# A two-layer decoder trunk on one core: matmul streams that take turns by whole chunks, an earlier weight load, and gates tied behind casts

## The chip, the cores and the metric

One NeuronCore of a Trainium2 chip runs the whole program. The metric is the device time of one execution in microseconds (us); lower is better. Before the change the median of three runs is 2906.79 us (2905.42 to 2907.09).

## The reference, cut to what matters

All matrices are float32; 256 positions, model width 2048, feed-forward width 5632.

```python
# layer 0
hn  = rmsnorm(h)
q, k, v, z, a, b, c_q, c_kv, k_rope = split_cols(hn @ w_in, L0_SPLITS)      # w_in: 2048 x 5200
y_a = gated_deltanet(q, k, v, z, a, b, ...)    # gates: sigmoid(b), softplus(a), cumulative decay
y_b = mla(c_q, c_kv, k_rope, cos, sin, ...)    # low-rank attention with rotary keys
h   = h + concat(y_a, y_b) @ w_out
h   = h + conv_ffn(rmsnorm(h))
h   = h + (p[0] @ w_proj) * sigmoid(rmsnorm(h) @ w_gate)
# layer 1: the same with retention in place of the mixer, then a final rmsnorm

def conv_ffn(hn, w_up, conv_w, conv_b, w_down):     # w_up: 2048 x 11264, w_down: 5632 x 2048
    u = causal_dwconv(hn @ w_up, conv_w) + conv_b   # width 3 along the positions
    gate, up = split(u, 2)
    return (silu(gate) * up) @ w_down
```

## The kernel before, in words

**Three matmuls for one.** Each float32 product is made of parts: a weight tile `raw` is cast to a rounded `hi` on ScalarE (L186) and the difference `lo = raw - hi` is taken on VectorE (L187). Activations are split the same way into tiles `xg`. TensorE then adds `hi` times both parts of x and `lo` times the high part. `cut` makes the casts and differences of one weight chunk; `split` takes a chunk that was loaded early from the list `ahead`, or loads one now through SyncE's DMA queue (L167), and cuts it. A chunk of weights is 1 MB (0.75 MB in the opening) and is cut into two `hi` and two `lo` tiles. There are four buffers for `raw`, four for `hi` and four for `lo`.

**Generators and steps.** The matmul loops are Python generators; each `yield` ends a step. `gemm_b` (up projection, transposed result) does a chunk of 1024 x 256 weights in three steps: 16 hi matmuls of 512 columns in two steps (L262), then 16 lo matmuls of 256 columns (L267); two chunks make one column block, which `joined` and `conv` then take through the causal convolution (L274 to L277, L1065, L1067). `gemm_a` does a chunk of 512 x 512 in three steps: 16 hi matmuls in two steps (L291, L292) and 8 lo matmuls (L297), all of 512 columns. After each step `turn()` runs one small deferred piece from the list `todo`, behind the last matmul.

**Order of issue.** The program's text gives the dependences and a priority. The framework in which it is written decides the order of the instructions on each engine by when its own model of the chip finds them ready; on the chip each engine then goes through its list in that order. `tc.issue_after(ins)` ties what is written inside it behind `ins` on the engine of `ins`.

**Feed-forward.** `ffn` goes over the 44 blocks of 128 hidden columns in groups: 4, then five times 8. While a group's `up` runs, the `down` of the group before it is worked off in turns with it. For four of the groups in each layer half of the output columns are done by `seven`: seven half-size products in place of eight (a fast-multiplication scheme), over sums of weight quadrants that GpSimd's accumulating DMA (L407) and two VectorE additions (L467) make. One `product` has three steps: two with four hi matmuls (L438, L439) and a cut each, one with four lo matmuls (L443). The other half of the columns is done by `plain`, four chunks of `gemm_a`. So `up` of a group has 48 steps, and the `down` beside it 12 plain and 21 product steps. `forms` are the sums of activation quadrants that the products need; they are made on VectorE (L376 to L384) each time two column pairs are ready.

Before, the two parts of `down` give one plain step, then two product steps, in turns; `up` first does `LAG` = 6 steps, and then after each single step of `up` the counter `owed` grows by `SHARE` = 0.85, and one step of `down` runs whenever it reaches 1.

**Opening.** The first product of layer 0 (16 blocks of x by 368 columns of `w_in`, four chunks) starts while x arrives. Its chunk 0 is loaded early into `ahead`; in the loop over the four column quarters of x, the two x tiles of the quarter after next are asked for at the loop's head, and the next chunk of weights only when `first_gemm` gets to it. `n0.feed` transposes x tiles (L311) and scales and splits them (L315, L316). Then come a second and a third product of the same kind (`g3` = 1 and 2). While they run, `turn()` works off `todo`: the scale's broadcast, two empty pieces, the five steps of `gates()` (L597 to L635: sigmoid, softplus, decay, with two changes of ScalarE's function table), a copy, the nine steps of `rope_steps` (L499 to L521), and so on. The results of a product are copied out of PSUM by `r_copy` (L576).

Of the kernel before, what the change touches and what calls it, by code (L numbers as in the profile page):

```python
# [13 lines left out]
F32 = mybir.dt.float32  # L14
# [16 lines left out]
WB = 4  # L31
PSA = 2
PSB = 4
LAG = 6
SHARE = 0.85
RATES = [1.7, 1.1, 1.1, 0.95, 2.8]
D = 2048
S = 256
# [2 lines left out]
CG = 4  # L41
# [43 lines left out]
def trunk(ctx: ExitStack, tc: tile.TileContext, a: dict):  # L85
# [12 lines left out]
    V, A, G, T = nc.vector, nc.scalar, nc.gpsimd, nc.tensor  # L98
    cnt = [0]

    def nm(s):
        cnt[0] += 1
        return f"{s}_{cnt[0]}"

    def t2(shape=(P, 512), dt=F32):
        return tp.tile(list(shape), dt, tag="t2", name=nm("t2"))
# [27 lines left out]
    def load_x(i, c, q=nc.sync):  # L134
        h[i][c] = t2()
        q.dma_start(h[i][c], a["x"][i * P : (i + 1) * P, c * 512 : (c + 1) * 512])
# [20 lines left out]

    grain = [GRAIN0]
    last_cast = [None]
    ahead = []  # L160

    def load(src, k, n, parts=1):
        raw = rawp.tile([P, k, n], F32, tag="raw", name=nm("raw"))
        rows = src.rearrange("(k p) n -> p k n", p=P)
        for q in range(0, k, k // parts):
            c = slice(q, q + k // parts)
            nc.sync.dma_start(raw[:, c], rows[:, c])  # L167
        return raw

    def split(src, k, n, views=None):  # L170
        raw = ahead.pop() if ahead else load(src, k, n)
        return cut(raw, k, n, views)

    def cut(raw, k, n, views=None):
        his, los = [], []
        step = max(1, PIECE // n)
        for k0 in range(0, k, step):
            kp = min(step, k - k0)
            hi = wp.tile([P, kp, n], F32R, tag="hi", name=nm("hi"))
            lo = wp.tile([P, kp, n], F32R, tag="lo", name=nm("lo"))  # L180
            rk = raw[:, k0 : k0 + kp]
            fine = max(1, grain[0] // n)
            for q in range(0, kp, fine):
                c = slice(q, min(q + fine, kp))
                for vi, vo in views or [(lambda t: t, lambda t: t)]:
                    last_cast[0] = A.copy(vo(hi)[:, c], vi(rk)[:, c])  # L186
                    V.tensor_sub(vo(lo)[:, c], vi(rk)[:, c], vo(hi)[:, c].bitcast(F32))  # L187
            his += [hi[:, i] for i in range(kp)]
            los += [lo[:, i] for i in range(kp)]
        return his, los  # L190
# [11 lines left out]
    def behind(step):  # L202

        with tc.issue_after(last_mm[0].ins):
            return step()

    def later(*steps):
        todo.extend(steps)

    def stepwise(gen, n):  # L210
        later(*[partial(next, gen, None)] * n)

    def turn():
        if todo:
# [38 lines left out]
    def gemm_b(w, c0, tiles):  # L253
        ps = pa()
        for c in range(2):
            hi, lo = split(w[c * 1024 : (c + 1) * 1024, c0 : c0 + 256], 8, 256)
            for j in range(2):
                for k in range(8):
                    x2, xh = xr(tiles, c * 8 + k)
                    wh = hi[k][:, j * P : (j + 1) * P]  # L260
                    first = c == 0 and k == 0
                    last_mm[0] = T.matmul(ps[:, j], wh, x2, start=first, stop=False)  # L262
                turn()
                yield
            for j in range(2):
                for k in range(8):
                    last_mm[0] = T.matmul(ps[:, j, :S], lo[k][:, j * P : (j + 1) * P], xr(tiles, c * 8 + k)[1], start=False, stop=c == 1 and k == 7)  # L267
            turn()
            yield
        return ps  # L270
# [259 lines left out]
    def idle(n):  # L530
        ps = pb()
        for _ in range(n):
            T.matmul(ps[:, :P], ones, ones, start=True, stop=True)
# [5 lines left out]
    w_in = a["l0_w_in"]  # L539
# [8 lines left out]
    n0.feed(0)  # L548
    idle(IDLE[1])
    for c in range(CG):  # L550
        if c < CG - 2:
            for i in range(NH):
                load_x(i, c + 2)
        next(first_gemm)
        if c > 0:
            with tc.issue_after(last_cast[0].ins):
                Norm.squares(n0, c - 1)
        if c < CG - 1:
            behind(partial(n0.feed, c + 1))
        for _ in range(2):  # L560
            next(first_gemm)
# [442 lines left out]
    n = Norm(C_NORM["l0_ffn_norm"])  # L1004
# [44 lines left out]
    def ffn(l, nf, nxt, aside=None):  # L1049
        pin = []  # L1050
        w_up, w_dn = a[f"l{l}_ffn_w_up"], a[f"l{l}_ffn_w_down"]
        fp = cp.tile([P, N_FFN], F32, name=nm("fp"), tag="fp")
        nc.sync.dma_start(fp, a["par"][:, N_PAR0 + l * N_FFN : N_PAR0 + (l + 1) * N_FFN])
        Xf = nf.tiles

        def fc(c):
            return fp[:, c : c + 1]

        def conv(cb, j0):
            ps = yield from gemm_b(w_up, cb, Xf)  # L1060
            u = joined(ps, nf.bc)
            y = t2((P, 2, S))
            for j in range(2):
                ct = j0 + j
                A.activation(y[:, j], u[:, j], AF.Identity, scale=fc(ct + 176), bias=fc(ct + 264))  # L1065
                for lag in range(1, 3):
                    V.scalar_tensor_tensor(y[:, j, lag:], u[:, j, : S - lag], fc(ct + (2 - lag) * 88), y[:, j, lag:], op0=ALU.mult, op1=ALU.add)  # L1067
            return y

        def up(g0, g1, tiles, forms):  # L1070
            kept = []
            for jp in range(g0, g1, 2):
                tiles.append(xtile())
                yg = yield from conv(jp * P, jp)
                yu = yield from conv(D_FF + jp * P, NFT + jp)
                A.activation(yg, yg, AF.Silu)
                V.tensor_mul(yg, yg, yu)
                put_split(tiles[-1], 0, 2, yg)
                if forms is not None:
                    kept.append(yg)  # L1080
                    if len(kept) == 2:
                        forms.add(*kept)
                        kept = []

        def down(g0, g1, tiles, forms, quads, then):
            r0, nk = g0 * P, g1 - g0

            def plain(cols):
                for c in cols:
                    ps = [pb() for _ in range(NH)]  # L1090
                    yield from gemm_a(w_dn, r0, nk, c * 512, 512, tiles, ps)
                    for i in range(NH):
                        V.tensor_add(h[i][c], h[i][c], ps[i])

            if forms is None:
                then()
                yield from plain(range(CG))
                return
            fast = seven(quads, tiles, forms, then)
            slow = plain(range(2, CG))  # L1100
            while next(slow, fast) is not fast:
                yield
                for _ in range(2):
                    if next(fast, slow) is not slow:
                        yield
            yield from fast

        groups = [(max(g - 4, 0), g + 4) for g in range(0, NFT, 8)]
        prev = None
        total = []  # L1110

        def following(g0):
            if g0 + 8 < NFT:
                if not total:
                    total.extend(running())
                quads.append(Quads(w_dn, g0 * P, 0, total))
                quads[-1].begin()

        quads = []
        for g0, g1 in groups:  # L1120
            forms = Forms() if 0 < g0 and g1 < NFT else None
            cur = (g0, g1, [], forms)
            going = up(g0, g1, cur[2], forms)
            if prev is not None:
                behind_it = down(*prev, quads[-1] if quads else None, partial(following, g0))
                for _ in range(LAG):
                    next(going)
                owed = 0.0
                for _ in going:
                    owed += SHARE  # L1130
                    while owed >= 1.0:
                        owed -= 1.0
                        next(behind_it, None)
                run(behind_it)
            else:
                run(going)
            if g0 == 4 and aside is not None:
                aside()
            if g1 + 8 == NFT:
                pin.append(ple_input(l))  # L1140
            prev = cur
        later(lambda: pin.append(ple_tiles(pin.pop())))
        run(proj_add(w_dn, [(prev[0] * P, prev[2], prev[1] - prev[0])], range(CG), nxt.feed))
        later(nxt.finish)
        return pin[0]
# [337 lines left out]
```

## Time and profile before

| | |
|---|---|
| median of three runs | 2906.79 us |
| profiled execution | 2905.5 us, span 2903.7 us |
| TensorE matmul (PE) busy | 2879.7 us, 15076 matmuls |
| TensorE weight load (PEld) busy | 2457.5 us |
| VectorE (DVE) busy | 2067.7 us |
| ScalarE (ACT) busy | 1539.3 us |
| DMA | 562.49 MB, mean 194 GB/s |
| granted TensorE clock, mean | 0.998 |

A line of the profile names an engine, a line of the kernel (L187), the operation, the tile written and those read, and a count. In a timeline the first two numbers are the start in us from the span's start and the length in us; a bracket at the end tells how long the engine stood idle before it, and what it waited for. Rows of matmuls are merged as `x16`, with the overlap of the last one in their length. "SPq" is SyncE's issue of a DMA. In the list of windows each row is one stretch: its length, then busy time and number of instructions of each engine, the granted TensorE clock as a share of full speed, and the DMA's share and rate.

### The profile page before, as it was taken

What the parts mean: (1) busy time and instruction counts of PE and PEld (TensorE: products, weight loads), DVE (VectorE), ACT (ScalarE), POOL (GpSimd) and SP (SyncE); (2) the same over time, 40 slices, a digit from 0 to 9 for tenths busy, and PEclk for the clock granted to TensorE, in tenths of its full rate; (3) what the DMA queues carried; (4) which work ended last, traced back from release to release, by engine and by line L of the source; (5) the groups of instructions that cost most, each with busy time, mean ns of one, the idle gap of its engine ahead of it and who ended that gap; (6) DMA issues with size and microseconds to landing.
All of it is one profiled execution on the core that took longest, in us unless ns stands there. A gap on an engine that the chain in (4) does not pass through costs nothing.

```text
span 2903.7 us, 38666 instructions
## 1 busy us (share of the span) xinstructions
PE 2879.7 (99%) x15076; PEld 2457.5 (85%) x15076; DVE 2067.7 (71%) x2898; ACT 1539.3 (53%) x2185; POOL 121.6 (4%) x116
## 2 busy tenths in 40 slices
PE   8999999999999999999999999999999999999998
PEld 8899988888888888888888888888888888888887
DVE  6878867777887877756565565655667878787865
ACT  6666655555555555554444444444545555555554
POOL 0111100000000000000000000000000000000000
PEclk9999999999999999999999999999999999999999
DMA  6444456657777777555555555555565777777654
GB/s 217 141 141 128 128 167 196 218 189 203 233 202 230 233 214 226 184 181 191 185 183 184 193 183 181 184 185 189 180 218 178 228 209 241 220 222 220 214 183 147
DMA packets 410040, 562.49 MB, mean 194 GB/s; under 512 B 10752, under 2 KB 266880, under 8 KB 409856
## 3 DMA queue, kind: packets, MB, share of 16 engines
q1 hardware_dynamic: 393376, 530.05, 55.8%
q0 software_dynamic: 13056, 25.17, 5.4%
q10 hardware_dynamic: 3424, 4.79, 0.5%
q8 instruction: 118, 1.93, 0.3%
q14 instruction: 66, 0.54, 0.1%
HBM read 557.87 MB, written 2.10 MB: 193 GB/s over the span
## 4 chain that ended last, share of the span: by engine, by line
PE 92%; DVE 4%; DMA 1%; issue 1%; ACT 1%; POOL 0%; SPq 0%; ACTq 0%; POOLq 0%; DVEq 0%
PE pa L262 28%; PE pa L267 15%; PE pa L291 10%; PE pa L292 10%; PE pa L297 10%; PE pb L292 2%; PE pb L291 2%; PE pb L297 2%; DVE lo L187 2%; PE pb L732 2%; PE pb L438 2%; PE pb L439 1%; PE pb L443 1%; PE pb L311 1%; DMA raw<-in_l_ffn_w_down_dram 1%
## 5 line engine op out<-in xcount | busy, mean ns | idle before, releaser
L187 DVE TENSOR_TENSOR lo<-raw,hi 128x1024 fp32r<-128x1024 f32 (+3 forms) x1140 | 1192.3, 1075 | 576.5 <-ACT hi L186 399.1
L186 ACT CAST hi<-raw 128x1024 fp32r<-128x1024 f32 (+3 forms) x1140 | 1014.4, 931 | 937.2 <-PE pa L292 327.9
L262 PE MATMUL pa<-xg,hi 128*128 128x512 f32 x3840 | 950.8, 393 | 0.0
L262 PEld LDWEIGHTS pa<-xg,hi 128*128 128x128 f32 x3840 | 705.8, 188 | 146.5 <-ACT hi L186 8.3
L291 PE MATMUL pa<-hi,xg 128*128 128x512 f32 (+1 forms) x1348 | 523.5, 389 | 7.2 <-ACT hi L186 7.1
L267 PEld LDWEIGHTS pa<-xg,lo 128*128 128x128 f32 x3840 | 495.0, 191 | 34.6 <-DVE lo L187 14.6
L292 PE MATMUL pa<-hi,xg 128*128 128x512 f32 (+1 forms) x1348 | 520.9, 387 | 0.3 <-DVE xg L316 0.2
L267 PE MATMUL pa<-xg,lo 128*128 128x256 f32 x3840 | 514.7, 284 | 1.5 <-DVE lo L187 1.2
L297 PE MATMUL pa<-lo,xg 128*128 128x512 f32 (+1 forms) x1348 | 332.6, 387 | 0.0
L291 PEld LDWEIGHTS pa<-hi,xg 128*128 128x128 f32 x1348 | 253.9, 188 | 56.9 <-ACT hi L186 7.7
L292 PEld LDWEIGHTS pa<-hi,xg 128*128 128x128 f32 x1348 | 254.0, 188 | 49.0 <-DVE xg L316 0.8
L297 PEld LDWEIGHTS pa<-lo,xg 128*128 128x128 f32 x1348 | 249.8, 188 | 47.5
L1067 DVE SCALAR_TENSOR_TENSOR t<-t,fp,t 128x255 f32<-128x255 f32 (+1 forms) x352 | 158.4, 480 | 54.1 <-ACT t L1065 50.7
L292 PE MATMUL pb<-hi,xg 128*128 128x512 f32 x348 | 135.9, 390 | 0.0
L291 PE MATMUL pb<-hi,xg 128*128 128x512 f32 x348 | 135.7, 390 | 0.0
L274 ACT COPY t<-pa 128x512 f32<-128x512 f32 x128 | 74.9, 585 | 100.9 <-PE pa L267 91.6
L1065 ACT ACTIVATE t<-t,fp 128x256 f32<-128x256 f32 x176 | 96.0, 593 | 48.0 <-DVE t L277 48.0
L407 POOL DMA_DIRECT2D xg<-in_l_ffn_w_down_dram x48 | 57.9, 1206 | 1185.4 <-DVE t L1067 395.5
L297 PE MATMUL pb<-lo,xg 128*128 128x512 f32 x348 | 92.4, 391 | 0.0
L275 DVE TENSOR_TENSOR t<-t,pa 128x512 f32<-128x512 f32 x128 | 87.1, 680 | 3.8 <-ACT t L274 3.8
L156 POOL TENSOR_TENSOR small<-small,mhalf 128x1 f32<-128x1 f32 (+2 forms) x38 | 28.6, 752 | 1415.3 <-DVE small L1252 622.6
L316 DVE SCALAR_TENSOR_TENSOR xg<-pb,par,xg 128x256 fp32r<-128x256 f32 x136 | 59.7, 479 | 35.9 <-ACT xg L315 35.5
(280 smaller groups left out, 2236.1 us busy)
## 6 DMA issues: line engine op xcount, KB each, us to landing
raw<-in_l_ffn_w_up_dram SPq DMA_DIRECT2D x176, 1024.0 KB, 5.6
raw<-in_l_w_in_dram SPq DMA_DIRECT2D x128, 1024.0 KB, 5.1
raw<-in_l_ffn_w_down_dram SPq DMA_DIRECT2D x56, 1024.0 KB, 5.3
raw<-in_l_w_out_dram SPq DMA_DIRECT2D x44, 1024.0 KB, 5.1
raw<-in_l_ffn_w_down_dram SPq DMA_DIRECT2D x64, 512.0 KB, 4.9
raw<-in_l_ple_gate_dram SPq DMA_DIRECT2D x32, 1024.0 KB, 5.1
xg<-in_l_ffn_w_down_dram POOLq DMA_DIRECT2D x48, 512.0 KB, 6.0
xg<-in_l_ffn_w_down_dram SPq DMA_DIRECT2D x16, 512.0 KB, 4.6
```

Of the source, the lines that this page charges most:

```text
L186: last_cast[0] = A.copy(vo(hi)[:, c], vi(rk)[:, c])
L187: V.tensor_sub(vo(lo)[:, c], vi(rk)[:, c], vo(hi)[:, c].bitcast(F32))
L262: last_mm[0] = T.matmul(ps[:, j], wh, x2, start=first, stop=False)
L267: last_mm[0] = T.matmul(ps[:, j, :S], lo[k][:, j * P : (j + 1) * P], xr(tiles, c * 8 + k)[1], start=False, stop=c == 1 and k == 7)
L274: A.copy(u, ps[:, :, S:])
L275: V.tensor_add(u, u, ps[:, :, :S])
L291: T.matmul(o[i], xh, hi[k], start=begin and k0 + k == 0, stop=False)
L292: last_mm[0] = T.matmul(o[i], xw, hi[k], start=False, stop=False)
L297: last_mm[0] = T.matmul(o[i], xl(tiles, k0 + k, i)[0], lo[k], start=False, stop=end and k0 + k == nkb - 1)
L316: V.scalar_tensor_tensor(t[:, kk, 1], pk, g, t[:, kk, 0].bitcast(F32), op0=ALU.mult, op1=ALU.subtract)
L1065: A.activation(y[:, j], u[:, j], AF.Identity, scale=fc(ct + 176), bias=fc(ct + 264))
L1067: V.scalar_tensor_tensor(y[:, j, lag:], u[:, j, : S - lag], fc(ct + (2 - lag) * 88), y[:, j, lag:], op0=ALU.mult, op1=ALU.add)
```

## The change

Four edits go together. (1) In `down`, the plain part and the product part take turns of `UNIT` = 3 steps, that is a whole chunk or a whole product: one plain, two products. (2) In the loop over groups, `down` gets its turn only after each third step of `up` (a whole up chunk), and then three steps of it; `LAG` is 2 chunks (6 steps as before) and `SHARE` 0.8. (3) In the opening, the next chunk of weights is loaded into `ahead` before the x tiles of the quarter after next; `ahead` becomes a queue that is taken from the left. (4) `cut` also keeps its last difference in `last_diff`, and `stepwise`, which serves `gates` and `rope_steps` in layer 0, ties each step behind the last cast on ScalarE and the last difference on VectorE that are written by then.

```diff
-LAG = 6
-SHARE = 0.85
+UNIT = 3
+LAG = 2
+SHARE = 0.8
...
-    ahead = []
+    last_diff = [None]
+    ahead = deque()
...
-        raw = ahead.pop() if ahead else load(src, k, n)
+        raw = ahead.popleft() if ahead else load(src, k, n)
...
-                    V.tensor_sub(vo(lo)[:, c], vi(rk)[:, c], vo(hi)[:, c].bitcast(F32))
+                    last_diff[0] = V.tensor_sub(vo(lo)[:, c], vi(rk)[:, c], vo(hi)[:, c].bitcast(F32))
...
     def stepwise(gen, n):
-        later(*[partial(next, gen, None)] * n)
+        def step():
+            with tc.issue_after(last_cast[0].ins), tc.issue_after(last_diff[0].ins):
+                next(gen, None)
+        later(*[step] * n)
...
     for c in range(CG):
+        if c < CG - 1:
+            ahead.append(load(w_in[(c + 1) * 512 : (c + 2) * 512, 4096 : 4096 + 368], 4, 368))
         if c < CG - 2:
             for i in range(NH):
                 load_x(i, c + 2)
...
             slow = plain(range(2, CG))
-            while next(slow, fast) is not fast:
-                yield
-                for _ in range(2):
-                    if next(fast, slow) is not slow:
-                        yield
-            yield from fast
+            going = True
+            while going:
+                going = False
+                for part in (slow, fast, fast):
+                    for _ in range(UNIT):
+                        if next(part, part) is not part:
+                            going = True
+                            yield
...
-                for _ in range(LAG):
+                for _ in range(LAG * UNIT):
                     next(going)
                 owed = 0.0
-                for _ in going:
+                for n, _ in enumerate(going, 1):
+                    if n % UNIT:
+                        continue
                     owed += SHARE
-                    while owed >= 1.0:
+                    if owed >= 1.0:
                         owed -= 1.0
-                        next(behind_it, None)
+                        for _ in range(UNIT):
+                            next(behind_it, None)
                 run(behind_it)
```

## The prediction

> **What bounds the kernel now.** I read the page first (engine shares, the chain that ended last), then windows by stage, then the timeline where PE pauses. A time is us from the span's start.
>
> ```profile
> span 2903.7 us, 38666 instructions
> ...
> PE 2879.7 (99%) x15076; PEld 2457.5 (85%) x15076; DVE 2067.7 (71%) x2898; ACT 1539.3 (53%) x2185; POOL 121.6 (4%) x116
> ...
> PE 92%; DVE 4%; DMA 1%; issue 1%; ACT 1%; POOL 0%; SPq 0%; ACTq 0%; POOLq 0%; DVEq 0%
> ```
>
> The matmul stream is the kernel: 92% of the chain is PE. No matmul is added or removed, so the change can only win the pauses in that stream or add new ones. The windows (span, busy time and count of PE, PEld, DVE, ACT, POOL; granted clock; DMA share; GB/s) show where pauses are dear:
>
> ```profile
> 0.00:30.00 30.00, 26.40 (x155) 24.49 (x156) 15.08 (x36) 19.33 (x50) 1.16 (x7) 1.00 0.87 289
> 30.00:36.00 6.00, 0.56 (x4) 0.25 (x2) 4.01 (x25) 5.27 (x13) 0.00 (x0) 0.78 0.01 3
> 36.00:41.00 5.00, 5.00 (x18) 4.82 (x19) 4.93 (x13) 3.42 (x9) 0.00 (x0) 0.58 0.37 103
> ...
> 734.65:866.79 132.14, 132.06 (x692) 111.51 (x692) 106.31 (x138) 73.95 (x91) 7.19 (x6) 1.00 0.76 223
> 866.79:999.06 132.27, 132.04 (x692) 111.50 (x692) 106.27 (x138) 73.85 (x91) 7.22 (x6) 1.00 0.75 223
> ...
> 2541.00:2673.00 132.00, 131.96 (x694) 111.71 (x693) 106.33 (x137) 73.90 (x90) 7.22 (x6) 1.00 0.76 225
> ```
>
> Two places stand out: an almost empty PE at 30 to 36 followed by a granted clock of 0.58, and the feed-forward groups, which repeat every 132 us, four times in each layer. Busy PE hides small pauses there, so I measure a group against plain up chunks that run alone:
>
> ```profile
> 516.04 3.82 PE L262 MATMUL pa<-xg,hi 128*128 128x512 f32 x16
> 519.70 2.08 PE L267 MATMUL pa<-xg,lo 128*128 128x256 f32 x16
> ...
> 538.31 3.82 PE L262 MATMUL pa<-xg,hi 128*128 128x512 f32 x16
> ```
>
> From 516.04 to 538.31 are four up chunks: 5.57 each. Sixteen 512-column matmuls start over 3.66, 0.229 each. A group holds 16 up chunks (89.1), 4 plain chunks of 24 and 7 products of 12 such matmuls (180 x 0.229 = 41.2): 130.3 without pauses. It takes 132.1, so it loses 1.9; eight groups lose 15.
>
> **Part 1: turns of whole chunks.** Call an up chunk U, a plain chunk S, a product F. By the rows, PE needs 5.57 for U, 24 x 0.229 = 5.5 for S, 2.75 for F. U and S fill two hi and two lo buffers out of four each, and so does F. With turns of single steps three chunks are open at once, six buffers' worth:
>
> ```profile
> 669.73 0.47 PE pa L267 x4
> 670.20 0.47 PE pb L443 x2
> 670.67 1.37 PE pa L262 x6
> ...
> 724.96 0.37 SPq L403
> 725.38 5.18 DMA raw<-in_l_ffn_w_down_dram
> 730.65 1.22 DVE raw L467
> ```
>
> This chain shows PE hopping between an up chunk's lo, a product's lo and an up chunk's hi, and later a late load for the sixth product. The timeline of DVE shows what that costs:
>
> ```profile
> 663.34 1.22 DVE L187 TENSOR_TENSOR lo<-raw,hi 128x1024 fp32r<-128x1024 f32 x1
> 670.77 1.23 DVE L187 TENSOR_TENSOR lo<-raw,hi 128x1024 fp32r<-128x1024 f32 x1 [6.22 <-PE pb L443]
> 673.37 1.22 DVE L187 TENSOR_TENSOR lo<-xg,hi 128x1024 fp32r<-128x1024 f32 x1 [1.37 <-PE pa L267]
> ```
>
> DVE, 80% busy in the group, stands idle 6.22 for a lo buffer of an unfinished product, then is late. With whole chunks only two are open, the four buffers hold the running one and the next, and this wait should go. Counts stay: 14 units after the lag x 0.8 gives 11 turns, 33 steps, the 12 S and 21 F steps there are; the order becomes U U, U, U S, U F, U F, U S, U, U F, U F, U S, U F, U, U F, U S, U F.
>
> What can be late next is DVE, by these rows of one group (count, busy, mean ns):
>
> ```profile
> L187 DVE TENSOR_TENSOR lo<-raw,hi 128x1024 fp32r<-128x1024 f32 x49 | 58.5, 1219 | 16.6 <-PE pb L443 7.0 <-issue 5.2 <-PE pa L267 2.5
> L1067 DVE SCALAR_TENSOR_TENSOR t<-t,fp,t 128x255 f32<-128x255 f32 (+1 forms) x32 | 14.4, 480 | 4.0 <-ACT t L1065 3.6
> L277 DVE TENSOR_TENSOR t<-t,rbc 128x512 f32<-128x512 f32 x8 | 5.5, 687 | 0.1
> ```
>
> The densest stretch is U F U F after the fourth convolution: PE 16.6; DVE eight differences (9.8), the convolution's end (2 x 0.69 + 4 x 0.48 = 3.3), gating and splitting it (two of 0.69: 1.4), the forms (six operations of at most 0.69, some 3), two adds to h (1.4): 18.9. DVE falls 2.3 behind, against a head start of up to two differences made during the U before and 3.66 of hi matmuls in each U. Left per group: between 0 and 1.9 or more. I take 0.6, nearer to the plain stretch above, where whole chunks in a row lose nothing: 8 x (1.9 - 0.6) = 10.4 won; bounds 15 won and, below, a loss.
>
> The other moved work is covered: the same weight loads of 5 us go out when a raw buffer's differences end, and with fewer chunks open the sixth product's load goes out two U earlier, 11 us (its cover gone, it costs the 1 us or so at 734). POOL's accumulations follow the first and fourth product and are read three products later, over 25 us. The next group's first quadrant sum now starts behind the last convolution's end; until its first product lie five U and an S, 33 us. Gone, either would cost F a transfer.
>
> **Part 2: second weights ahead of x.**
>
> ```profile
> 5.42 2.36 SPq L136 DMA_DIRECT2D t<-in_x_dram  x4
> ...
> 7.83 2.01 SPq L167 DMA_DIRECT2D raw<-in_l_w_in_dram  x3
> ...
> 13.00 1.52 PE L297 MATMUL pa<-lo,xg 128*128 128x368 f32 x8
> 15.60 1.70 ACT L186 CAST hi<-raw 128x368 fp32r<-128x368 f32 x4 [2.25 <-DMA raw<-in_l_w_in_dram]
> ...
> 16.15 0.44 PE L291 MATMUL pa<-hi,xg 128*128 128x368 f32 x1 [1.64 <-ACT hi L186]
> ...
> 17.80 1.03 PE L311 MATMUL pb<-ident,t 128*128 128x128 f32 x8
> ```
>
> SP issues four x tiles, then the weights, whose landing ends the cast's wait. Issued at 5.42 instead of 7.83 they should land 2.4 earlier, some 13.2, before PE is through with chunk 0 at 14.5. The pause of 1.64 goes: 1.7 with the slow restart (bounds 0 and 2.0). Late next: the x tiles for the transposes at 17.80, behind one more load. At 289 GB/s its 128 x 4 x 368 words take 2.6; the transposes show no wait now, and about 1 could come back.
>
> **Part 3: gates behind casts.**
>
> ```profile
> 30.74 0.55 ACT L576 ACTIVATE t<-pa,small 128x352 f32<-128x352 f32 x1
> ...
> 31.33 0.56 ACT L576 ACTIVATE t<-pa,small 128x352 f32<-128x352 f32 x1
> 31.48 0.17 DVE L597 SCALAR_TENSOR_TENSOR small<-slab 128x16 f32<-128x16 f32 x1 [1.18 <-ACT slab L576]
> ...
> 32.44 1.28 ACT L621 ACT_TABLE_LOAD   x1
> ...
> 33.97 1.28 ACT L626 ACT_TABLE_LOAD   x1
> ...
> 35.37 3.28 ACT L186 CAST hi<-raw 128x368 fp32r<-128x368 f32 x8
> ...
> 35.91 0.67 PE L291 MATMUL pa<-hi,xg 128*128 128x368 f32 x1 [5.44 <-ACT hi L186]
> ```
>
> On ACT the gates with two table loads stand between the copies out of the first product (until 31.9) and eight casts that wait for nothing else (DMA share 0.01). Behind those casts, the first cast begins at 31.9 and PE, as now 0.54 behind it, at 32.4: 1.9 of the idle time stays, 3.5 is won. The slow clock goes too: (1 - 0.58) x 5 = 2.1. Together 5.6; bounds 0 and 7.5 (casts ahead of the copies as well). Queued behind the gates are then chunk 2's casts: ACT ends eight casts at 35.2, DVE eight differences near 36; the gate chain took 2.5 from 31.48 to its logarithm, so it ends near 39, and PE, with two chunks of 24 matmuls before it (8 took 1.52 or less above, so about 4 each), wants chunk 2 near 40.5. Cover about 1.5; if the second table load goes in between as well, it costs up to 0.6. The rope steps, also tied, have a chunk's time each: nothing.
>
> The clock was 0.78 over 30 to 36, so it fell near 33.4, 2.9 after the last matmul; a pause of 1.64 at 16 left it at 1.00. I take no fall for 1.9; a fall would give back 2.1. [...]
>
> **Sum.** 10.4 + 1.7 + 5.6 = 17.7 off the profiled execution's 2905.5: 2887.8. The median of the three runs, 2906.8, is 1.3 above it: 2889.
>
> **Rivals.** (a) Issue follows readiness, not the text: PE's hops at 669 to 672 cut even single steps, so chunks may stay mixed and the groups keep their 15. Only the opening wins 7.3: 2899. Against it: fewer chunks are offered at once. (b) The opening wins, and DVE's bursts add up to 1 per group: 2901 to 2909, no change that can be told (0.2%, 5.8 us, is what a measurement of this kernel can tell). (c) Slower: F's lo is late. F has 8 x 0.229 = 1.83 of hi matmuls to cover two differences of 1.22. If they start only as F starts, because DVE's queue holds a convolution's end first, each F waits 0.6 and 0.1 to restart: 56 x 0.7 = 39, less 15 and 7.3: 2923. It decides from 0.4 per F. For it: 18.9 against 16.6; against it: F's buffers are free a whole U earlier.
>
> [...]
>
> **Chances.** Forecast 0.58 (alone 2880 to 2896), (a) 0.18, (b) 0.12, (c) 0.12. Faster 0.76, same 0.12, slower 0.12. All bounds won, 15 + 2.0 + 7.5, give 2882; with some spread the range starts at 2880 and ends at 2905, inside (b), leaving out (c) and half of (b).
>
> **What would show it.** Groups of 130.5 to 131 instead of 132.1; no DVE wait of 6 for a product's lo; PE runs of 16 up matmuls; L291's first pause under 0.3 near 14.5, its second under 2.5; clock 1.00 from 30 to 41. It is wrong if lo weight loads of products wait for DVE, if groups stay at 132, or if chunk 2 of the second product stalls behind gates.

## The result and the profile after

The changed kernel takes 2880.51 us (median of four runs, 2879.16 to 2880.76); the kernel before, on the same chip, 2906.94 (2905.42 to 2907.42). The ratio is 0.9909, with a 95% interval of 0.9892 to 0.9926: 26.4 us by the medians. The profiled executions differ by 24.9 (2905.5 to 2880.6, spans 2903.7 to 2878.8). The forecast was 2889, range 2880 to 2905: the direction and the largest part are right, the size is 8 us short and the result lies at the range's lower edge, below the 2882 that all of the prediction's upper bounds make together.

The lines of the kernel after stand a few numbers further down: cast L188, difference L189, up hi L267 and lo L272, `gemm_a` L296, L297 and L302, products L443, L444 and L448, copies out of the first products L583, gates L604 to L638.

The page of the kernel after, the lines that answer to those of before:

```profile
span 2878.8 us, 38652 instructions
...
PE 2860.8 (99%) x15076; PEld 2464.2 (86%) x15076; DVE 2060.9 (72%) x2898; ACT 1537.8 (53%) x2185; POOL 121.8 (4%) x116
...
PE 98%; DVE 1%; ACT 0%; DMA 0%; issue 0%; POOL 0%; ACTq 0%; POOLq 0%; DVEq 0%
```

The matmuls are the same 15076, and the chain that ended last is now 98% PE, not 92%. PE's busy time fell by 18.9 as well, though no matmul went: a group of before was 132.06 busy for the matmuls that take 129.87 now, so short pauses counted as busy there. So it is not the busy time that has to be read but the length of a stage. The windows of the kernel after:

```profile
0.00:30.00 30.00, 25.80 (x156) 24.19 (x156) 15.35 (x37) 20.20 (x55) 1.16 (x7) 1.00 0.84 290
30.00:36.00 6.00, 5.55 (x22) 5.17 (x23) 5.01 (x18) 4.91 (x16) 0.00 (x0) 0.72 0.42 126
36.00:41.00 5.00, 5.00 (x32) 5.00 (x31) 2.96 (x10) 4.96 (x10) 0.00 (x0) 1.00 0.50 157
725.93:855.80 129.87, 129.87 (x693) 112.49 (x692) 105.29 (x137) 73.67 (x90) 7.20 (x6) 1.00 0.76 227
855.80:985.67 129.87, 129.87 (x694) 112.49 (x692) 105.36 (x137) 73.67 (x90) 7.22 (x6) 1.00 0.76 228
2520.05:2649.92 129.87, 129.87 (x694) 112.50 (x693) 105.48 (x138) 73.67 (x90) 7.22 (x6) 1.00 0.76 229
```

The empty stretch at 30 to 36 is nearly full; the clock still falls, but earlier and for a shorter time (0.72 here, 1.00 from 36). The three groups shown take 129.87 each, in both layers; before, the three shown took 132.14, 132.27 and 132.00. All eight, from the first up matmul of a group to that of the next, take 129.87 to 129.89 after and 132.12 to 132.45 before, 132.27 on the mean.

Taking the same matmul in both traces by its place in PE's order, its start after minus its start before shows where the 24.9 went:

| point | after minus before, us |
|---|---|
| 21 us (opening, second chunk under way) | -1.9 |
| 45 us (gates and first casts over) | -5.7 |
| 599 us (in layer 0's feed-forward, ahead of the groups with products) | -5.6 |
| after layer 0's feed-forward | -15.3 |
| 2193 us (in layer 1's feed-forward, ahead of the groups with products) | -15.2 |
| end | -24.9 |

So: weights 1.9, gates 3.8, turns 9.65 and 9.7. Nothing of it is given back between the feed-forwards.

The first part of each feed-forward wins nothing, though its turns changed too. From 486.5 to 643.6 us of the kernel before, `up` runs alone and then takes turns with `plain`, single steps, two chunks open (PE's timeline of the kernel before):

```profile
553.10 1.98 PE L262 MATMUL pa<-xg,hi 128*128 128x512 f32 x8
554.91 1.98 PE L297 MATMUL pb<-lo,xg 128*128 128x512 f32 x8
```

Here an up chunk is interrupted by a plain chunk's lo part. The 157.07 us of this stretch are 157.03 in the kernel after, where chunks run whole, and the list of waits has no row of PE or PEld in either kernel for as long as the two streams take turns. The loss begins where the products join, that is, with the third open chunk.

PE's order in a group of the kernel after (PE's timeline, merged rows):

```profile
734.67 3.79 PE L267 MATMUL pa<-xg,hi 128*128 128x512 f32 x16
738.30 2.08 PE L272 MATMUL pa<-xg,lo 128*128 128x256 f32 x16
740.21 3.82 PE L267 MATMUL pa<-xg,hi 128*128 128x512 f32 x16
743.87 2.08 PE L272 MATMUL pa<-xg,lo 128*128 128x256 f32 x16
745.78 0.40 PE L443 MATMUL pb<-hi,t 128*128 128x512 f32 x1
...
747.62 1.07 PE L448 MATMUL pb<-lo,t 128*128 128x512 f32 x4
748.53 3.79 PE L267 MATMUL pa<-xg,hi 128*128 128x512 f32 x16
```

Whole up chunks of 16 and 16, then a whole product. The same place in the kernel before:

```profile
731.65 0.64 PE L267 MATMUL pa<-xg,lo 128*128 128x256 f32 x4
732.12 0.63 PE L443 MATMUL pb<-lo,t 128*128 128x512 f32 x2
732.59 1.76 PE L297 MATMUL pb<-lo,xg 128*128 128x512 f32 x7
734.65 1.69 PE L267 MATMUL pa<-xg,lo 128*128 128x256 f32 x12 [0.29 <-DVE lo L187]
```

Here an up chunk, a product and a plain chunk are in their lo parts at once, and PE waits for the next difference. In the list of waits (us in total, times, longest) of one group of the kernel before, these rows stand for that, among others:

```profile
DVE lo L187 <- PE pb L443: 7.0, 2, 6.2
...
PEld pa L267 <- DVE lo L187: 2.0, 4, 0.7
```

In the group at 725.93 of the kernel after, no row of PE's or PEld's is in the list at all, and none of DVE waiting for a product's matmuls. DVE's longest is this:

```profile
DVE lo L189 <- ACT hi L188: 15.2, 9, 2.5
```

DVE waits for casts, that is, it is ahead of its work.

### The profile page after: what moved, and what is told of

It is laid out like the page before. It is cut to its first block, busy times and chain, and to the rows that moved or that the text cites. A ratio compares the mean times of both kernels' runs of the same rounds, so it can differ in the third digit from the quotient of the medians.

```text
span 2878.8 us, 38652 instructions
## 1 busy us (share of the span) xinstructions
PE 2860.8 (99%) x15076; PEld 2464.2 (86%) x15076; DVE 2060.9 (72%) x2898; ACT 1537.8 (53%) x2185; POOL 121.8 (4%) x116
## 4 chain that ended last, share of the span: by engine, by line
PE 98%; DVE 1%; ACT 0%; DMA 0%; issue 0%; POOL 0%; ACTq 0%; POOLq 0%; DVEq 0%
PE pa L267 30%; PE pa L272 16%; PE pa L297 10%; PE pa L296 10%; PE pa L302 10%; PE pb L297 3%; PE pb L296 3%; PE pb L302 3%; PE pb L444 2%; PE pb L443 2%; PE pb L448 2%; PE pb L739 2%; PE pb L316 1%; PE pa L936 1%; PE pb L745 0%; PE pb L1234 0%
## 5 line engine op out<-in xcount | busy, mean ns | idle before, releaser
L189 DVE TENSOR_TENSOR lo<-raw,hi 128x1024 fp32r<-128x1024 f32 (+3 forms) x1140 | 1197.9, 1075 | 555.8 <-ACT hi L188 498.8
L188 ACT CAST hi<-raw 128x1024 fp32r<-128x1024 f32 (+3 forms) x1140 | 1010.0, 931 | 955.5 <-PE pa L297 327.6
L267 PE MATMUL pa<-xg,hi 128*128 128x512 f32 x3840 | 925.9, 392 | 0.0
L267 PEld LDWEIGHTS pa<-xg,hi 128*128 128x128 f32 x3840 | 709.7, 188 | 140.6 <-DVE xg L321 0.3
L296 PE MATMUL pa<-hi,xg 128*128 128x512 f32 (+1 forms) x1348 | 522.8, 388 | 2.0 <-ACT hi L188 1.9
L297 PE MATMUL pa<-hi,xg 128*128 128x512 f32 (+1 forms) x1348 | 521.4, 387 | 0.3 <-DVE xg L321 0.2
L272 PEld LDWEIGHTS pa<-xg,lo 128*128 128x128 f32 x3840 | 490.3, 191 | 16.3
L272 PE MATMUL pa<-xg,lo 128*128 128x256 f32 x3840 | 502.0, 283 | 0.0
L302 PE MATMUL pa<-lo,xg 128*128 128x512 f32 (+1 forms) x1348 | 331.7, 386 | 0.0
L296 PEld LDWEIGHTS pa<-hi,xg 128*128 128x128 f32 x1348 | 253.9, 188 | 50.5 <-ACT hi L188 2.2
L297 PEld LDWEIGHTS pa<-hi,xg 128*128 128x128 f32 x1348 | 253.7, 188 | 49.4 <-DVE xg L321 0.8
L302 PEld LDWEIGHTS pa<-lo,xg 128*128 128x128 f32 x1348 | 250.1, 188 | 47.9
L297 PE MATMUL pb<-hi,xg 128*128 128x512 f32 x348 | 135.9, 391 | 0.0
L296 PE MATMUL pb<-hi,xg 128*128 128x512 f32 x348 | 135.8, 390 | 0.0
L302 PE MATMUL pb<-lo,xg 128*128 128x512 f32 x348 | 86.5, 389 | 0.0
```

The source lines that it names most:

```text
L189: last_diff[0] = V.tensor_sub(vo(lo)[:, c], vi(rk)[:, c], vo(hi)[:, c].bitcast(F32))
L296: T.matmul(o[i], xh, hi[k], start=begin and k0 + k == 0, stop=False)
L297: last_mm[0] = T.matmul(o[i], xw, hi[k], start=False, stop=False)
L302: last_mm[0] = T.matmul(o[i], xl(tiles, k0 + k, i)[0], lo[k], start=False, stop=end and k0 + k == nkb - 1)
```

## The experiments

Each stands beside the kernel before on the same chip. "Cost" is against the kernel before of that row, by medians; the ratio stands with its 95% interval.

| run | median us | kernel before | cost us | ratio (95%) |
|---|---|---|---|---|
| e1_turns | 2886.43 | 2906.44 | -20.0 | 0.9935 (0.9920 to 0.9951) |
| e2_weights | 2903.43 | 2906.44 | -3.0 | 0.9991 (0.9982 to 1.0000) |
| e3_gates | 2902.22 | 2906.44 | -4.2 | 0.9985 (0.9976 to 0.9994) |
| e4_next_first | 2878.25 | 2906.44 | -28.2 | 0.9905 (0.9892 to 0.9919) |
| e5_after_again | 2880.70 | 2906.00 | -25.3 | 0.9912 (0.9898 to 0.9925) |
| e6_next_again | 2879.08 | 2906.00 | -26.9 | 0.9907 (0.9893 to 0.9920) |
| e7_down_units | 2880.66 | 2906.00 | -25.3 | 0.9912 (0.9898 to 0.9925) |
| e8_up_units | 2907.41 | 2906.00 | +1.4 | 1.0006 (0.9997 to 1.0015) |
| e9_six_buffers | 2889.70 | 2906.82 | -17.1 | 0.9944 (0.9929 to 0.9958) |
| e10_fewer_tiles | 2909.52 | 2906.82 | +2.7 | 1.0012 (1.0002 to 1.0021) |
| e11_five_raw | 2908.39 | 2906.82 | +1.6 | 1.0004 (0.9994 to 1.0013) |
| e12_twice | 2881.22 | 2906.82 | -25.6 | 0.9913 (0.9897 to 0.9930) |

### The turns alone

The kernel after with the opening and the gates of before:

```diff
-        if c < CG - 1:
-            ahead.append(load(w_in[(c + 1) * 512 : (c + 2) * 512, 4096 : 4096 + 368], 4, 368))
...
-        def step():
-            with tc.issue_after(last_cast[0].ins), tc.issue_after(last_diff[0].ins):
-                next(gen, None)
-        later(*[step] * n)
+        later(*[partial(next, gen, None)] * n)
```

> The changed kernel with the opening as it was before: x tiles ahead of the second weights, gates free of the casts. Only the turns of whole chunks are left of the change. Theory (each part gives what its own stage shows: turns 19, weights 1.9, gates 3.8): some 2887.6, that is 19.3 less than before, with feed-forward groups of about 129.8 us and the 5.4 us pause near 30 back, with a slow clock after it. Rival (the opening's gain is larger, because it moves the phase of everything behind it): over 2890.

20.0 less. By the trace it is never more than 0.2 from the kernel before until the two streams of the feed-forward take turns, 0.05 ahead at 599 us and 19.4 ahead at the end; its groups take 129.87 to 129.89. The turns, then, are worth 19 to 20, all of it in the groups with products.

### The weights alone

The kernel before with the loads of the next chunk ahead of the x tiles:

```diff
-    ahead = []
+    ahead = deque()
...
-        raw = ahead.pop() if ahead else load(src, k, n)
+        raw = ahead.popleft() if ahead else load(src, k, n)
...
+        if c < CG - 1:
+            ahead.append(load(w_in[(c + 1) * 512 : (c + 2) * 512, 4096 : 4096 + 368], 4, 368))
```

> The kernel before with one edit, the next weights loaded ahead of the x tiles. Theory: the pause near 16 (1.64 us) goes and nothing comes back, 1.9 less than before: 2905.0. Rival (the pause is only moved to the x tiles' transposes, as the DMA is full there): within 0.5 of before.

3.0 less by medians, at the edge of what the interval can tell from nothing. By the trace it is 1.86 ahead at 21 us, 2.5 at 45 and 2.2 at the end. The 30-us pause is still there, 5.38 long, but the low clock after it lasted 3.41, not 6.83: that is the difference between 1.86 and 2.5. No transpose came late for the load put ahead of its x tiles: the 1 us that I thought could come back did not.

### The gates alone

The kernel before with the tied steps:

```diff
+    last_diff = [None]
...
-                    V.tensor_sub(vo(lo)[:, c], vi(rk)[:, c], vo(hi)[:, c].bitcast(F32))
+                    last_diff[0] = V.tensor_sub(vo(lo)[:, c], vi(rk)[:, c], vo(hi)[:, c].bitcast(F32))
...
-        later(*[partial(next, gen, None)] * n)
+        def step():
+            with tc.issue_after(last_cast[0].ins), tc.issue_after(last_diff[0].ins):
+                next(gen, None)
+        later(*[step] * n)
```

> The kernel before with one edit, gates and rope steps tied behind the last cast and difference. Theory A (the pause shrinks from 5.4 to 1.9, and the clock falls all the same, for one window or two): 3.6 to 3.9 less than before, 2903.1, with a granted clock under 1.0 somewhere between 31 and 41. Theory B (the recorded prediction: a pause of 1.9 leaves the clock alone, and the fall in the changed kernel had to do with the moment at which its pause came): 5.6 less, 2901.3, clock 1.0 from 30 to 41.

4.2 less by medians, 3.3 to 3.5 by the trace: it lost 0.57 in the opening (the pause for the second weights was 1.97 long here, 1.64 in the trace of before) and won 3.84 between 30 and 45 us. The pause falls from 5.44 to 1.86, and the clock falls all the same. The windows of this run:

```profile
13.21:16.62 3.41, 1.54 (x10) 1.23 (x8) 0.90 (x2) 0.84 (x3) 0.00 (x0) 1.00 1.06 385
30.27:33.68 3.41, 1.54 (x9) 1.05 (x7) 1.42 (x4) 2.54 (x8) 0.00 (x0) 1.00 0.01 4
33.68:37.10 3.42, 3.42 (x12) 3.21 (x11) 3.39 (x12) 2.67 (x8) 0.00 (x0) 0.50 0.34 78
```

From 33.68 the granted clock is 0.50, for 3.42, after a stretch of the same length in which PE was busy for 1.54. The expectation with the fall, 2903.1, is 0.9 off the median, the one without it, 2901.3, also 0.9; the trace, not the time, decides for the fall. The first row is a stretch with the same busy time that was not followed by a fall: see the last section.

### The next product's first step ahead of the copies

What the tied steps leave of the pause is the copies out of the first product, which stand ahead of the casts on ACT. The kernel after, with the first step of the next product written ahead of them:

```diff
+    gemm = first_gemm
...
-        ps = run(first_gemm if g3 == 0 else gemm_a(w_in, 0, KB, 4096 + 368 * g3, 368, X))
+        ps = run(gemm)
+        if g3 < 2:
+            gemm = gemm_a(w_in, 0, KB, 4096 + 368 * (g3 + 1), 368, X)
+            next(gemm)
```

> The changed kernel with one more edit in the opening: the first step of the next 368-column product (its first casts and eight matmuls) is written ahead of the copies out of the product before. Theory: the pause of 1.9 us near 30 goes and with it the slow clock behind it (about 1.9 us, eleven matmuls and the broadcast at half speed): 3 to 4 less than the changed kernel, 2877. Rival (the copies and the scale's root set the order, so the pause comes back at the next PSUM tile or later): within 1 of the changed kernel, 2880.5.

It was run twice, the second time beside another run of the kernel after:

> The changed kernel itself, on the chip of the runs beside it. Both theories: 26 us less than before. It is here for the direct comparison with the next kernel and for one more look at the clock: the pause of 1.9 near 29 should be there, and if the clock falls by free-running windows of 3.41 us whose phase changes from run to run, the fall comes only where one window holds nearly all of the pause.

> The kernel with the next product's first step ahead of the copies, again, now beside the changed kernel on one chip. Theory: 1.5 to 2.5 less than the changed kernel (the traces say 1.7), clock at 1.0 from 10 us on. Rival (the earlier difference lay between chips): within 0.7 of the changed kernel.

2878.25 and 2879.08 against 2880.51 and 2880.70: 1.6 less in the pair that shares a chip and its runs of the kernel before, 1.7 to 2.6 by the spans (2877.1 and 2876.3 against 2878.8 and 2878.9). That is less than the 3 to 4 expected, and less than the 0.2% that a pair of runs can tell. The traces say why. Against the kernel after, both runs win 3.85 between 28 and 42 us, as expected. The pause and the fall are gone, in both runs; windows of e4_next_first:

```profile
30.00:36.00 6.00, 6.00 (x37) 5.95 (x36) 4.75 (x21) 5.11 (x15) 0.00 (x0) 1.00 0.58 163
36.00:41.00 5.00, 4.39 (x28) 4.12 (x27) 2.90 (x10) 4.56 (x11) 0.00 (x0) 1.00 0.69 232
```

But PE lost 0.61 in the second row, where it had lost nothing, and by the starts of its matmuls 0.85 is given back there. PE's timeline there:

```profile
38.97 0.33 PE L296 MATMUL pa<-hi,xg 128*128 128x368 f32 x1
39.91 0.37 PE L637 MATMUL pb<-slab 128*128 128x16 f32 x2 [0.60 <-issue]
```

and that of all engines just before:

```profile
37.25 1.28 ACT L633 ACT_TABLE_LOAD   x1
...
38.54 0.21 ACT L633 ACTIVATE small<-alog 128x8 f32<-128x8 f32 x1
...
39.18 0.54 DVE L189 TENSOR_TENSOR lo<-raw,hi 128x368 fp32r<-128x368 f32 x1 [1.29 <-ACT hi L188]
39.63 0.17 DVE L634 SCALAR_TENSOR_TENSOR slab<-small,small 128x16 f32<-128x16 f32 x1
```

PE stands before the gates' matmuls (L637), which read what DVE writes at 39.63 (L634). That operation had what it reads at 38.75, but stood in DVE's queue behind a difference that waited for a cast, and the cast, which began at 38.66, stood behind the table load on ACT. So the tie that brought the casts forward now holds up the gates, as soon as PE is early enough to notice. Another 0.6 is given back in small steps behind that, most of it before 100 us; where from is open. It is still the fastest of the kernels, by a little.

### Which of the turns does it

The change makes both sides whole: the up chunks and the two parts of `down`. One at a time:

```diff
# e7_down_units: the kernel after, with before's loop over the up steps
-LAG = 2
-SHARE = 0.8
+LAG = 6
+SHARE = 0.85
...
-                for n, _ in enumerate(going, 1):
-                    if n % UNIT:
-                        continue
+                for _ in going:
                     owed += SHARE
-                    if owed >= 1.0:
+                    while owed >= 1.0:
                         owed -= 1.0
-                        for _ in range(UNIT):
-                            next(behind_it, None)
+                        next(behind_it, None)
```

> The changed kernel, but after each single step of the up projection comes 0.85 of a step of the down projection again (lag of 6 steps); only the down projection's own two parts take turns by whole chunks. So two chunks are open at once, not three. Theory (open chunks fill the four buffers, and pauses grow with their number): part of the gain, the groups between 130.2 and 131.3 us, in all 4 to 13 more than the changed kernel. Rival (the late load and the differences' order within a product were the cause, and are mended by this half): within 2 of the changed kernel.

```diff
# e8_up_units: the kernel after, with before's turns inside `down`
-            going = True
-            while going:
...
+            while next(slow, fast) is not fast:
+                yield
+                for _ in range(2):
+                    if next(fast, slow) is not slow:
+                        yield
+            yield from fast
```

> The changed kernel, but the down projection's two parts again give one plain and two product steps in turns; a whole up chunk then three such steps. A plain chunk and a product stay open across up chunks: three open at once. Theory: the gain is mostly lost, groups of 131.3 us or more, 12 to 25 more than the changed kernel. Rival (it is enough that up chunks run whole): within 4 of the changed kernel.

e7_down_units: 2880.66, equal to the kernel after run beside it (2880.70), with groups of 129.87. I had expected 4 to 13 more; the rival's number, within 2, came true, but e11_five_raw below speaks against the late load that it names as the cause. Its up steps still alternate with those of `down`. PE's timeline:

```profile
784.05 2.08 PE L272 MATMUL pa<-xg,lo 128*128 128x256 f32 x16
...
787.80 1.98 PE L267 MATMUL pa<-xg,hi 128*128 128x512 f32 x8
789.62 1.98 PE L302 MATMUL pb<-lo,xg 128*128 128x512 f32 x8
791.43 1.98 PE L267 MATMUL pa<-xg,hi 128*128 128x512 f32 x8
```

An up chunk opens at 787.80 while a plain chunk has its lo part ahead of it, and is done half by half: two chunks open, and no pause. e8_up_units, with whole up chunks but a plain chunk and a product open side by side, loses the whole gain of the turns: 2907.41, 26.7 more than the kernel after. Its group:

```profile
726.69:860.10 133.41, 132.78 (x693) 110.96 (x692) 105.56 (x139) 74.04 (x91) 7.23 (x6) 1.00 0.75 221
```

133.41 is even over the 132 of before, and in its list of waits for that group the rows of before are back:

```profile
DVE lo L189 <- PE pb L448: 5.0, 2, 3.6
...
PEld pa L272 <- DVE lo L189: 4.0, 9, 1.0
```

So it is the turns inside `down` that cost, that is the third open chunk, and not the cutting up of the up chunks. Nor is it the number of changes from one stream to another: in layer 0's four groups PE's order falls into 300 pieces in e7_down_units and 216 in the kernel after (a piece is a row of matmuls of one stream, all hi or all lo), for the same 129.87.

### More buffers instead of fewer open chunks

If three open chunks fail for want of buffers, six hi and six lo buffers should cure the kernel before with its text untouched. Room for them comes from the pool of `t` tiles, so a control has the smaller pool alone:

```diff
# e9_six_buffers                # e10_fewer_tiles: only this line
-T2B = 27                       -T2B = 27
+T2B = 19                       +T2B = 19
...
-WB = 4
+WB = 6
```

> The kernel before, single steps in turns, but six hi and six lo buffers, room for three open chunks; the 16 KB come from the pool of 128x512 tiles, 19 in place of 27. Theory (the pauses come from three chunks sharing four buffers): most of them go, groups of 129.8 to 130.6, in all 10 to 18 less than before. Rival (the order of differences or late loads make them): groups of 131.5 or more, within 4 of before.

> The control for the run with six buffers: the kernel before with 19 in place of 27 tiles of 128x512 and nothing else. Both theories: within 4 of before; if it is much slower, the run with six buffers is read against this one.

17.1 less than the kernel before, and 19.8 less than the control, which is what the turns alone won (20.0). A group of e9_six_buffers:

```profile
734.45:864.32 129.87, 129.87 (x695) 112.51 (x694) 105.86 (x138) 73.38 (x91) 7.20 (x6) 1.00 0.77 227
```

The same 129.87 with the turns of single steps; only the fourth group of each layer stays at 130.4. The order of the text was not wrong in itself; it asked for two buffers more than there were. PE's own order, though, is not that of before: with four buffers it cuts many steps (the rows of x4, x2 and x7 at 731.65) and falls into 405 pieces, with six most steps are whole and there are 301. So the run does not tell the wait for a buffer on the chip from the order that the framework chose for four buffers; the shortage stands behind both.

### Is it the late load?

The chain of before also showed a late load and a wait for a raw tile. One raw buffer more, with the order of before:

```diff
-T2B = 27
+T2B = 23
...
-RAWB = 4
+RAWB = 5
```

> The kernel before with five raw buffers for loads in place of four (the 8 KB come from the pool of 128x512 tiles, 23 in place of 27). Theory (four hi and lo buffers are what binds): only the pause at a group's end goes, which follows the sixth product's late load, up to 4 less than before. Rival (late loads behind held raw buffers make the pauses): 8 or more less than before.

2908.39 against 2906.82, and groups of 131.84 to 133.00, 132.06 on the mean against 132.27: by this trace a fifth raw tile is worth 0.2 of the 2.4 that a group lost. The median hides that gain, since the trace is 4.9 behind the kernel before when the groups begin, with two falls of the clock that before has not (at 17.7 and 383 us).

### Is DVE next?

My sum left 0.6 in each group for DVE running late. Here the products' differences are computed twice, in the kernel after (the second writes the same values):

```diff
-    def cut(raw, k, n, views=None):
+    def cut(raw, k, n, views=None, twice=False):
...
-                    last_diff[0] = V.tensor_sub(...)
+                    for _ in range(1 + twice):
+                        last_diff[0] = V.tensor_sub(...)
...
-                hi, lo = cut(right[q], 2, 512)
+                hi, lo = cut(right[q], 2, 512, twice=True)
```

> The changed kernel with each difference of a product's chunk computed twice, 14 x 1.22 = 17 us more of VectorE in a group of 130, some 123 busy. It asks how near VectorE is to the bound. Theory 1 (as recorded: the stretch U F U F asks for more than PE's time already): pauses of 2 us or more per group, 16 or more above the changed kernel. Theory 2 (with two chunks open the head start carries such bursts): at most 4 above it.

2881.22, 0.7 over the kernel after, which ran on another chip. A group of it:

```profile
724.51:854.62 130.11, 130.11 (x694) 112.36 (x693) 120.58 (x152) 73.55 (x90) 7.19 (x6) 1.00 0.76 226
```

15.3 us more work for DVE (120.58 for 105.29, 93% of the group) lengthen the group by 0.24; the eight take 130.00 to 130.20, 0.2 more on the mean, 1.7 in all. The profiled span, 2878.8, is that of the kernel after only because this run's clock did not fall in the opening (see the last section), which won 1.6. DVE is no bound near the 81% of the changed kernel.

## Why the prediction was right or wrong

**The mechanism was right.** The pauses came from three open chunks on four hi and four lo buffers, and an order with two open chunks has none. e8_up_units (three open, four buffers: 133.4), e7_down_units (two open: 129.87) and e9_six_buffers (three open, six buffers: 129.87) show it from both sides, and so does the stretch of the kernel before with two open (157.07 against 157.03). One half of the reading was too broad: I took whole up chunks as part of it, and by e7_down_units and e8_up_units they bring nothing.

**The turns' term was mis-sized: 10.4, measured 19.35 in the trace and 20.0 by e1_turns.** Two steps of it failed.

First, the length of a group with and without pauses. I took four up chunks that run alone as the zero, at 5.57 each, which makes 130.3; it is 129.87. In the rows of the kernel after, from 734.67 to 745.78, an up chunk behind a product takes 5.54, and the next, behind another up chunk, 5.57. Most up chunks of a group stand behind a product or a plain chunk, so my zero was some 0.02 too long in each, and 16 of those are most of the difference of 0.43. The groups of before, on the other hand, take 132.27 on the mean, a little over the 132.1 that I read. So before lost 2.4 per group, not 1.9: 8 x 2.4 = 19.2, which is nearly all of the 19.35.

Second, the residual of 0.6 per group (4.8 in eight) for DVE's dense stretches. I summed DVE's work over U F U F, 18.9 against PE's 16.6, and set a head start of two differences against it without counting out how far DVE runs ahead in the up chunks before. In the kernel after, no row of PE or PEld is in the list of waits, and in e12_twice 15.3 us more on DVE lengthen a group by only 0.2. A sum over the densest stretch says that a buffer is drawn down, not that it runs dry.

**The weights** were put at 1.7 and measured 1.9. L302's lo matmuls of chunk 0 go over into the second chunk's hi matmuls with no gap (PE's timeline of the kernel after), where a pause of 1.64 had been:

```profile
13.22 1.52 PE L302 MATMUL pa<-lo,xg 128*128 128x368 f32 x8
14.57 0.33 PE L296 MATMUL pa<-hi,xg 128*128 128x368 f32 x1
```

**The gates** were put at 5.6, 3.5 of pause and 2.1 of clock; measured 3.8. The pause did what was forecast: 1.86 were left (1.9 forecast), and the casts begin behind the last copy. All engines' timeline, the rows of ACT and PE:

```profile
29.45 0.56 ACT L583 ACTIVATE t<-pa,small 128x352 f32<-128x352 f32 x1
29.88 3.30 ACT L188 CAST hi<-raw 128x368 fp32r<-128x368 f32 x8
...
30.45 0.43 PE L296 MATMUL pa<-hi,xg 128*128 128x368 f32 x1 [1.86 <-ACT hi L188]
```

The clock step failed: "I take no fall for 1.9". It fell at 31.26 for 3.41, and the windows of the kernel after show both:

```profile
27.85:31.26 3.41, 1.54 (x9) 1.03 (x8) 0.83 (x2) 2.58 (x8) 0.00 (x0) 1.00 0.04 13
31.26:34.67 3.41, 3.41 (x12) 3.23 (x11) 3.38 (x12) 2.62 (x8) 0.00 (x0) 0.50 0.34 73
34.67:38.10 3.43, 3.43 (x22) 3.43 (x22) 1.68 (x10) 3.12 (x7) 0.00 (x0) 1.00 1.00 349
```

The prediction had the other branch as well ("a fall would give back 2.1", and 5.6 less that is 3.5), and that is the one that came: 3.8. The choice rested on one pause of 1.64 that left the clock at 1.00; with a pause of 1.86 it fell in four runs (after, e3_gates, e5_after_again, e7_down_units) and stayed in e8_up_units (see the last section). The slow time of before, 6.83, was halved, not removed. That chunk 2 of the second product comes late behind the gates did not happen: its casts slip in between the gates' instructions and table loads on ACT, at 34.95, 35.47 and 37.39, and PE shows no pause there.

**The rivals.** (a), an order that stays mixed, fell with the runs of 16; (b) and (c), DVE's bursts and a late lo of the products, with the empty list of PE's waits: the lo tiles of the products are made early enough.

**The sum** by its own terms, forecast and measured: turns 10.4 and 19.35, weights 1.7 and 1.9, gates 5.6 and 3.8; 17.7 and 25.05, against 24.9 between the two profiled spans. Of the 9 us by which the turns were undersized, about 3.5 are the zero of the group, 5 the residual, and the rest mostly the length of a group before; the clock's 2 went the other way. The turns went beyond their own bound of 15, so it was luck that the total stayed in the range: by half a microsecond, and by the 2 us of spread below 2882.

## What to carry to other kernels

When several weight streams share a ring of buffers, count how many chunks the order keeps open at once and compare that with the ring: one chunk too many cost 2.4 us in each group of 130 here, and either fewer open chunks or two more buffers of each kind won all or nearly all of it. Before taking a busy engine as the next bound, ask how far it can run ahead of its consumer; at 81% busy no wait of the matmul stream for DVE shows, and at 93% a group was only 0.2 us longer. Where a pause is measured by comparing with a stretch that runs freely, look for a second such stretch with the same neighbours, since 0.02 in each chunk was 2.6 us in the sum (16 chunks, eight groups).

## What the runs showed of the hardware

**Each fall of the clock came a whole number of 3.41 us after its last rise.** Counted from the moment that the granted clock rose to 1.00, before fell after 27.307 us (6.04 to 33.35) and the kernel after too (3.96 to 31.26), 8 times 3.4134; e5_after_again, 4.45 to 31.75 (8); e7_down_units, 6.48 to 30.38 (7). At the end of the program it fell once more, in before 837 times 3.4134 after the rise (40.17 to 2897.13), in the kernel after 831 times (34.67 to 2871.15). In e11_five_raw the falls at 17.73 and 382.96 lie 107 times that length apart. I call a stretch of this length, counted from a rise or a fall, a window. Ahead of the end, the low clock lasted one window, 3.41 (after, e2_weights, e3_gates, e5_after_again, e7_down_units, e10_fewer_tiles, and the three of e11_five_raw), or two, 6.83 (before, e1_turns, e9_six_buffers). Two windows of before, the one of its pause and the next:

```profile
29.93:33.34 3.41, 0.54 (x4) 0.23 (x2) 2.23 (x18) 2.65 (x8) 0.00 (x0) 1.00 0.01 5
33.34:36.76 3.42, 0.85 (x3) 0.85 (x4) 2.62 (x11) 3.38 (x8) 0.00 (x0) 0.50 0.00 0
```

My reading of before, a fall 2.9 after the last matmul, was a chance distance to the end of a window.

**A pause of 1.86 was followed by a fall where it lay within one window, and by none where a window ended in it.** It lay within one in the kernel after (28.59 to 30.45, window 27.85 to 31.26), e3_gates, e5_after_again and e7_down_units. In e8_up_units the opening is that of the kernel after, its pause also 1.86 long, but a window ended at 29.38 in the middle of it:

```profile
25.97:29.38 3.41, 2.41 (x15) 2.10 (x13) 0.80 (x4) 0.90 (x4) 0.71 (x1) 1.00 0.18 64
29.38:32.79 3.41, 2.55 (x13) 2.19 (x14) 2.57 (x6) 3.41 (x9) 0.00 (x0) 1.00 0.01 2
```

Two windows with PE busy for 2.4 and 2.6, and no fall. e12_twice opens in the same way (2.40 and 2.56), without a fall. e8_up_units won 7.4 in the opening and e12_twice 7.3, e5_after_again 5.5 with the same opening and a fall: by these three a fall of one window cost some 1.9. So the same opening differed by about 2 us with where a window happened to end.

PE did not stand idle for the whole of such a window: windows in which it was busy for 1.54 or 1.55 of 3.41 were followed by a fall four times (after, e3_gates, e5_after_again, e7_down_units), and one with 1.72 once (e11_five_raw).

**What stays open.** PE's busy time alone does not decide. In the windows of these traces with the full clock, a busy time of 1.12 us or less was always followed by a fall and one of 1.77 or more never (1.12: e11_five_raw, 14.32 to 17.73; 1.77: before, 12.87 to 16.28, with the pause of 1.64 in it), but in between it went both ways: in e3_gates the window from 13.21 to 16.62 had PE busy for the same 1.54, and no fall came. Nor is it the DMA share, which was high in that window (1.06 against 0.01). In e11_five_raw a fall came behind the first and the third of these windows, and none behind the second:

```profile
14.32:17.73 3.41, 1.12 (x7) 0.70 (x6) 0.60 (x2) 1.13 (x3) 0.00 (x0) 1.00 1.06 377
31.39:34.80 3.41, 1.54 (x10) 1.23 (x8) 1.48 (x9) 1.67 (x7) 0.71 (x1) 1.00 0.23 84
379.55:382.96 3.41, 1.72 (x9) 0.98 (x8) 3.37 (x8) 1.51 (x4) 0.00 (x0) 1.00 0.24 64
```

What else the clock goes by, no run here tells.
